# A two-block transformer on one core: gates onto all partitions through DRAM, two norm rows by DMA, four modulation units moved

## The chip, the core and the metric

The kernel runs on one core of one Trainium2 chip. Its engines are TensorE (PE, with its weight loads as PEld), VectorE (DVE), ScalarE (ACT), GpSimd (POOL) and SyncE (SP), beside sixteen DMA engines. The metric is the device time in microseconds, the median of several runs. The profile comes from one profiled execution.

## What is computed

Input x has 256 tokens of width 1024, everything in fp32. Two blocks follow each other.

The first block has two layers. For each layer the conditioning vector c gives six rows of width 1024:

```
mod = silu(c) @ w_ada[layer] + b_ada[layer]
shift_m, scale_m, gate_m, shift_f, scale_f, gate_f = split(mod, 6)
h = rms_norm(x, g_mix) * (1 + scale_m) + shift_m
x = x + gate_m * (concat(conv, sgu, gla, hgrn mixers of h @ w_in) @ w_out)
h = rms_norm(x, g_ffn) * (1 + scale_f) + shift_f
x = x + gate_f * y        # layer 0: swiglu; layer 1: 8 experts, top 2
```

After the second layer comes `rms_norm(x, final_norm_g)`. The second block is a forgetting attention (its norm has the gain `a_norm_2`), a convolutional feed-forward, a sparse attention and a second convolutional feed-forward. The diff touches how the gates `gate_m`, `gate_f` and the two gains `final_norm_g`, `a_norm_2` come onto all 128 partitions, and when the last modulation rows are computed.

## The kernel before, in words

All work is written out in one order, and each engine runs its own instructions in that order. Tokens lie in two tiles of 128 partitions. Every fp32 product is made from a high and a low part of both operands in three matmuls (`mm3`); ScalarE casts the high part of a weight half (L266) and VectorE subtracts it to get the low part (L267). The weights come as units of 1 MB in one stream on SP's queue (`Stream`): six raw buffers, freed in order, and at most four split halves. In the experts four more raw buffers and two row tiles are lent to the stream.

The stages are the first mixers (layer 0), a dense feed-forward, the second mixers (layer 1), the experts, then the second block. `mixers` runs twelve projections of 256 columns (`unit`, `tok_unit`), and between them the chains of the two linear attentions (`linear`), mostly on VectorE and ScalarE. `project` and `close` apply w_out, add the residual and start the next norm; `close` has two gaps in which `fill` is called.

The modulation is computed by `ada(l, g)` for layer l and a third g of the six rows, from eight units of w_ada that are used as they are. One unit is four matmuls with 32 output partitions each (L781). After the eighth unit the group ends: ScalarE copies the PSUM bank into a row (L786), PE transposes it (L789), and VectorE makes shift and scale columns (`modc`, `gs`, L791 and L797). For g > 0 one gate row is left. The tile for it is loaded with the bias on all partitions by a DMA of GpSimd (L370); PE broadcasts the gate from one partition of the row to all 128 by two matmuls with a column of the identity (L806), and VectorE adds each to the bias in place (L809). The gates are read in the residual of `project` and of the feed-forward (L1102), and the last one in the experts' `scatter` (L1419).

Group (0,0) is made at the start. The others, (0,1), (0,2), (1,0), (1,1), (1,2), are 40 units, and `FILL` (L341) says how many are taken at each call of `fill`: the twelve calls of the first mixers, the two gaps after them, the feed-forward, the two gaps after it, the twelve calls of the second mixers. `plan` puts the units' loads into the stream in the same places. A group holds one of the eight PSUM banks from its first unit to its end. Group (1,2) gives the shift and scale that `routing` spreads before the experts, and the gate that the experts use.

Row tiles (tag "row", three of them) hold gates, the decay rows of `linear` (L938, L939), and later the two norm rows. `experts` runs eight experts of seven chunks; at the fifth chunk of the last one it calls `late`, which is `spread` of the two gains: per row eight broadcast matmuls against the identity (L385) and two ScalarE copies (L387). `combined` reads the rows after the last expert (L1620, L1647). GpSimd has little else to do: the routing weights (L1216), four products at the end of the second mixers (L1278) and a few splits (L267).

Of the kernel before, what the change touches and what calls it, by code (L numbers as in the profile page):

```python
# [9 lines left out]
FT = mybir.dt.float32  # L10
# [5 lines left out]
OP = mybir.AluOpType  # L16
AX = mybir.AxisListType
P = 128
T = 256
D = 1024  # L20
# [51 lines left out]
def _vec(v):  # L72
    return np.asarray(v).reshape(-1, P).T
# [44 lines left out]
def vectors(a):  # L118
    c = Cols()
    c.add("c", _vec(a["c"]))  # L120
    for l in range(2):
        c.add(f"mixg{l}", _vec(a["norm_mix_g"][l]))
        c.add(f"bada{l}", _vec(a["b_ada"][l]))
        c.early = c.early or c.n
        c.add(f"ffng{l}", _vec(a["norm_ffn_g"][l]))
        c.add(f"convw{l}", a["conv_w"][l].reshape(3, 2, P).transpose(2, 1, 0))
        c.add(f"glab{l}", _vec(a["gla_b_gate"][l]))
        c.add(f"glag{l}", _twice(a["gla_norm_g"][l]))
        c.add(f"hgg{l}", _twice(a["hgrn_norm_g"][l]))
        c.add(f"lb{l}", _vec(a["hgrn_lower_bounds"][l]))  # L130
        c.add(f"glaw{l}", a["gla_w_gate"][l])
        c.add(f"fb{l}", _vec(a["f_conv_b_2"][l]))
        c.add(f"fw{l}", a["f_conv_w_2"][l].reshape(3, 44, P).transpose(2, 1, 0))
    c.add("fing", _vec(a["final_norm_g"]))
    c.add("ag", _vec(a["a_norm_2"]))
    for n, s in (("aq", "a_q_gain_2"), ("ak", "a_k_gain_2"), ("kc", "kc_gain_2"), ("ks", "ks_gain_2"),
                 ("kw", "kw_gain_2"), ("bq", "b_q_gain_2")):
        c.add(n + "gain", _twice(a[s]))
    f = np.asarray(a["a_b_f_2"]).reshape(16, 1)
    c.add("fbias", np.concatenate([f, np.zeros_like(f), f]))  # L140
    c.add("gbias", np.asarray(a["b_b_gate_2"]).reshape(48, 1))
    for n in ("kc", "vc"):
        c.add(n + "pe", a[n + "_pe_2"].reshape(16, 2, 64).transpose(1, 2, 0).reshape(P, 16))
    return c
# [2 lines left out]
SHAPES = {n: np.zeros(s, np.float32) for n, s in dict(  # L147
    c=(1, D), norm_mix_g=(2, D), norm_ffn_g=(2, D), b_ada=(2, 6 * D), conv_w=(2, 3, 256), gla_b_gate=(2, P),
    gla_norm_g=(2, 64), hgrn_norm_g=(2, 64), hgrn_lower_bounds=(2, 256), gla_w_gate=(2, 16, P), f_conv_b_2=(2, 5632), f_conv_w_2=(2, 3, 5632),
    final_norm_g=(D,), a_norm_2=(1, D), a_q_gain_2=(1, 64), a_k_gain_2=(1, 64), kc_gain_2=(64,), ks_gain_2=(64,), kw_gain_2=(64,), b_q_gain_2=(1, 64),  # L150
    kc_pe_2=(32, 64), vc_pe_2=(32, 64), a_b_f_2=(1, 16), b_b_gate_2=(1, 48)).items()}

EARLY_UP = (0, 11)
# [6 lines left out]
def pack(a):  # L160

    a = {k: np.asarray(v) for k, v in a.items()}
    o = {"x": a["x"].reshape(T, D), "w_ada": a["w_ada"]}
    o["consts"] = constants().array()
    o["vecs"] = vectors(a).array()
    w = a["w_in"]
    o["w_in"] = np.stack([
        np.concatenate([_ws(w[l][:, s + (_PAIRS if s in _FEAT[:2] else np.arange(256))]) for s in _FEAT]
                       + [_ts256(w[l][:, s:s + 256]) for s in _TOK])
        for l in range(2)])  # L170
    o["w_ag"] = np.stack([_kcol(w[l][:, 1792:1808]) for l in range(2)])
    rows = np.concatenate([np.arange(512), 512 + _PAIRS, 768 + _PAIRS])
    o["w_out"] = np.stack([_ts1024(a["w_out"][l][rows]) for l in range(2)])
    o["sgu_w"] = a["sgu_w"].transpose(0, 3, 1, 2)
    o["rows_b"] = a["b_ada"]
    o["sgu_g"] = a["sgu_norm_g"]
    o["sgu_b"] = a["sgu_b"]
    o["bg"], o["fg"] = a["b_norm_2"], a["f_norm_2"]
    o["kvg"] = a["kv_norm_2"].reshape(1, D)
    o["ffn1"], o["ffn3"] = _first256(a["ffn_w1"][0], 0), _first256(a["ffn_w3"][0], 0)  # L180
    o["ffn2"] = _ts1024(a["ffn_w2"][0])
    o["router"] = _kcol(a["moe_router"][0])
    for n in ("1", "3"):
        w = a["moe_w" + n][0].reshape(NE, 2, 4, P, 7, 512).transpose(0, 4, 1, 3, 2, 5)
        o["moe" + n] = w.reshape(NE, 14, P, 2048)
    o["moe2"] = a["moe_w2"][0].reshape(NE, 14, 2, P, D).transpose(0, 1, 3, 2, 4).reshape(NE, 14, P, 2048)
    w = a["a_w_in_2"][0]
    o["a_in"] = np.concatenate([_ws(w[:, :2048]), _ts256(w[:, 2048:3072])])
    o["a_f"] = _kcol(np.concatenate([w[:, 3072:], np.zeros_like(w[:, 3072:]), w[:, 3072:]], 1))
    o["a_out"] = _ts1024(a["a_w_out_2"][0])  # L190
    w = a["kv_w_2"].reshape(D, 6, P)
    o["kv_w"] = np.concatenate([_ts256(w[:, 0:2].reshape(D, 256)), _ws(w[:, [2, 4]].reshape(D, 256)),
                                _ts256(w[:, [3, 5]].reshape(D, 256))])
    for n in ("kc", "vc"):
        o[n + "_w1"] = a[n + "_w1_2"].reshape(16, P, 256).transpose(1, 0, 2)
        o[n + "_w2"] = _kcol(a[n + "_w2_2"])
    w = a["b_w_in_2"][0]
    o["b_in"] = _ws(w[:, :D].reshape(D, 2, 8, 64).transpose(0, 2, 1, 3).reshape(D, D))
    o["b_g"] = _kcol(w[:, D:])
    o["b_out"] = _ts1024(a["b_w_out_2"][0].reshape(2, 8, 64, D).transpose(1, 0, 2, 3).reshape(D, D))  # L200
    w = a["f_w_up_2"]
    o["f_up"] = np.stack([_first256(w[l], *EARLY_UP) for l in range(2)])
    o["f_dn"] = np.stack([_ts1024(a["f_w_down_2"][l]) for l in range(2)])
    o["pos"] = a["positions_2"].reshape(1, T)
    return {k: np.ascontiguousarray(v) for k, v in o.items()}
# [132 lines left out]
class Core:  # L338
    TAIL = 4

    FILL = [1, 1, 1, 1, 1, 1, 1, 2, 2, 2, 2, 1], [2, 2], [0] * 2 + [1] * 16 + [0] * 4, [2, 2], [0] * 12  # L341

    def __init__(self, ctx, tc, a, out, stop=None):
        self.ctx, self.tc, self.nc, self.a, self.out, self.stop = ctx, tc, tc.nc, a, out, stop
        pool = lambda name, **k: ctx.enter_context(tc.tile_pool(name=name, **k))
        self.raw = pool("raw", bufs=Stream.RAW)
        self.split = pool("split", bufs=Stream.SPLIT)
        self.keep = pool("keep", bufs=1)
        self.nrm = pool("nrm", bufs=1)
        self.part = ExitStack()  # L350
        self.mine = self.part.enter_context(tc.tile_pool(name="first", bufs=1, side="right"))
        self.psum = pool("psum", bufs=8, space=bass.MemoryType.PSUM)
        self.s = Stream(self.nc, self.raw, self.split)
        self.names = 0
        self.open = self.between = None
        self.own = None
# [8 lines left out]
    def row(self, ap):  # L365

        self.names += 1
        t = self.mine.tile([P, D], FT, name=f"row{self.names}", tag="row", bufs=3)
        if ap is not None:
            self.nc.gpsimd.dma_start(t, ap.partition_broadcast(P).rearrange("p a d -> p (a d)"))  # L370
        return t

    def warm(self, n):

# [395 lines left out]
    def ada(self, l, g):  # L770

        nc = self.nc
        ps = self.ps("ada")
        for k in range(8):
            if k < 7:
                t, = self.s.whole()
            else:
                with self.s.quiet():
                    t, = self.s.whole()
            for j in range(4):  # L780
                nc.tensor.matmul(ps[32 * j:32 * j + 32, :], self.cT[:, k:k + 1].to_broadcast([P, 32]), t[:, j * 512:(j + 1) * 512],  # L781
                                 start=k == 0, stop=k == 7)
            if k < 7:
                yield
        row = self.rows()[1][:, :512]
        nc.scalar.copy(row, ps)  # L786
        tr = self.ps("adt")
        for b in range(4):
# [1 line left out]
        o = 16 * g  # L790
# [3 lines left out]
        if g == 0 or g == 2:  # L794
            n = g // 2
# [2 lines left out]
                                           self.vv(("mixg", "ffng")[n] + str(l)), op0=OP.add, op1=OP.mult)  # L798
        if g > 0:

            v = 2 if g == 1 else 5
            j0 = 0 if g == 1 else 2
            gate = self.row(self.a["rows_b"][l:l + 1, v * D:(v + 1) * D])
            for h in range(2):
                gp = self.ps("gate")
                nc.tensor.matmul(gp, self.cc("ident")[:, 32 * (j0 + h):32 * (j0 + h) + 1].to_broadcast([P, P]), row,  # L806
                                 start=True, stop=True)
                c = slice(h * 512, (h + 1) * 512)
                nc.vector.tensor_tensor(gate[:, c], gp, gate[:, c], op=OP.add)  # L809
            self.gate[l, g] = gate  # L810
        yield

# [1456 lines left out]
    def run(self):  # L2269
        nc, tc, a, s = self.nc, self.tc, self.a, self.s  # L2270
# [7 lines left out]
        first = self.normed(self.feats(self.gs[:, 0, 0], self.modc[:, 0, 0:8], 1))  # L2278
# [21 lines left out]
        for l in range(2):  # L2300
# [7 lines left out]
            rows = self.project(y, self.gate[l, 1], then, (2, 3, 0, 1, 6, 7, 4, 5), between, gap=fill, close=self.close_routed if l else None)  # L2308
# [15 lines left out]
                nc.scalar.dma_start(self.router, a["router"])  # L2324
        first = self.late
        done, last = self.combined(*first)
        self.experts(*rows, lambda: [self.spread(r, self.vv(n)) for r, n in zip(first, ("fing", "ag"))], done)
        if self.stopped("ffn1"):
            return
        self.phase("fox", c64=8, c1024=4, c1536=8, c2048=12, c8192=3, spare=((8192, 1), (2048, 3)))  # L2330
# [11 lines left out]
        rows = self.conv_ffn(0, self.feats(self.row(a["kvg"]), early=2), kT)  # L2342
# [33 lines left out]
```

## Time and profile before

| | |
|---|---|
| median of 3 runs | 2280.06 us (2277.39 to 2282.93) |
| profiled execution, its own time | 2279.25 us |
| its span, first to last instruction | 2277.5 us |
| instructions | 34045 |
| PE busy | 2206.2 us (97%) |
| DVE busy | 1749.1 us (77%) |
| ACT busy | 1409.4 us (62%) |
| POOL busy | 66.8 us (3%) |
| HBM read | 580.76 MB, 255 GB/s over the span |

Times in the views count from the start of the span. Busy is the time in which an engine executes; idle before an instruction is put down to what released it last. A matmul's record is longer than the time for which it keeps the next one waiting, since matmuls are pipelined: the spacing of starts tells what one costs. An fp32 matmul shows as two records.

### The profile page before, as it was taken

How to read it: one execution, taken by the hardware profiler on the slowest of the kernel's cores; microseconds unless marked ns; L12 is line 12 of the kernel's file. 1: busy time of each engine (PE TensorE's matmuls, PEld its weight loads, DVE VectorE, ACT ScalarE, POOL GpSimd, SP SyncE). 2: the span in 40 equal slices, each digit the busy share in tenths (PEclk: the TensorE clock that was granted, in tenths of full speed). 3: DMA queues.
4: the chain of work that ended last, by engine and by line, in shares of the span. 5: the costliest groups of instructions: out<-in, count | busy, mean ns of one | idle time of the engine just before them, and what ended most of it. 6: DMA issues, size and time to landing. Idle time of an engine off the chain costs nothing. (4 is left out here: it accounts for less than half of the span.)

```text
span 2277.5 us, 34045 instructions
## 1 busy us (share of the span) xinstructions
PE 2206.2 (97%) x13348; PEld 1841.1 (81%) x13348; DVE 1749.1 (77%) x2284; ACT 1409.4 (62%) x1956; POOL 66.8 (3%) x104
## 2 busy tenths in 40 slices
PE   6999999999999999999999999998999999999999
PEld 4777888887887878787887878786888998779998
DVE  3675445586989899989999899887677777676776
ACT  3544334545877777777777777676665556555554
POOL 1000000001000000000000000001004000100000
PEclk9999999999999999999999999999999999999999
DMA  9767766535999999999999999686334555313451
GB/s 394 274 243 288 271 246 219 196 105 209 359 369 348 347 339 365 348 354 347 350 367 352 337 350 362 231 342 242 130 112 160 204 185 193 132 38 130 167 191 68
DMA packets 87560, 584.35 MB, mean 257 GB/s; under 512 B 9984, under 2 KB 11648, under 8 KB 20960
## 3 DMA queue, kind: packets, MB, share of 16 engines
q1 hardware_dynamic: 84096, 575.22, 68.2%
q0 software_dynamic: 1296, 4.59, 0.6%
q8 instruction: 106, 1.74, 0.3%
q10 hardware_dynamic: 2000, 2.29, 0.3%
q14 instruction: 62, 0.51, 0.1%
HBM read 580.76 MB, written 1.05 MB: 255 GB/s over the span
## 5 line engine op out<-in xcount | busy, mean ns | idle before, releaser
L267 DVE TENSOR_TENSOR lo<-raw,hi 128x1024 fp32r<-128x1024 f32 x695 | 834.5, 1225 | 292.5 <-ACT hi L266 282.6
L266 ACT CAST hi<-raw 128x1024 fp32r<-128x1024 f32 x698 | 719.7, 1050 | 328.2 <-PE fu L441 152.2
L440 PE MATMUL fu<-hTh,hi 128*128 128x256 f32 x1440 | 413.1, 287 | 2.0 <-DVE lst L933 1.2
L442 PE MATMUL fu<-hTh,lo 128*128 128x256 f32 x1440 | 408.0, 283 | 0.8 <-DVE lo L267 0.8
L441 PE MATMUL fu<-hTl,hi 128*128 128x256 f32 x1440 | 407.8, 283 | 0.0
L440 PE MATMUL h<-hi,xh 128*128 128x512 f32 x896 | 361.1, 403 | 4.3 <-PEq L1521 4.2
L441 PE MATMUL h<-lo,xh 128*128 128x512 f32 x896 | 354.4, 396 | 4.5 <-DVE lo L267 4.5
L442 PE MATMUL h<-hi,xl 128*128 128x512 f32 x896 | 354.8, 396 | 0.0
L440 PEld LDWEIGHTS fu<-hTh,hi 128*128 128x128 f32 x1440 | 274.1, 190 | 17.3 <-issue 12.2
L441 PEld LDWEIGHTS fu<-hTl,hi 128*128 128x128 f32 x1440 | 272.5, 189 | 3.2 <-issue 2.2
L267 DVE TENSOR_TENSOR lo<-more,hi 128x1024 fp32r<-128x1024 f32 x216 | 258.1, 1222 | 21.3 <-ACT hi L266 18.3
L442 PEld LDWEIGHTS fu<-hTh,lo 128*128 128x128 f32 x1440 | 272.0, 189 | 1.0 <-DVE lo L267 1.0
L266 ACT CAST hi<-more 128x1024 fp32r<-128x1024 f32 x216 | 224.1, 1052 | 44.3 <-PE h L442 22.4
L441 PEld LDWEIGHTS h<-lo,xh 128*128 128x128 f32 x896 | 168.9, 189 | 45.2 <-DVE lo L267 7.9
L440 PEld LDWEIGHTS h<-hi,xh 128*128 128x128 f32 x896 | 168.8, 188 | 41.9 <-ACT yh L1421 4.7
L442 PEld LDWEIGHTS h<-hi,xl 128*128 128x128 f32 x896 | 168.6, 188 | 41.3
L440 PE MATMUL y<-hi,egh 128*128 128x512 f32 x448 | 177.4, 396 | 0.7 <-ACT egh L454 0.7
L442 PE MATMUL y<-hi,egl 128*128 128x512 f32 x448 | 177.4, 396 | 0.0
L441 PE MATMUL y<-lo,egh 128*128 128x512 f32 x448 | 176.4, 394 | 0.8 <-DVE lo L267 0.8
L441 PE MATMUL acc<-lo,gh 128*128 128x512 f32 x264 | 104.6, 396 | 1.7 <-DVE lo L267 1.7
L440 PE MATMUL acc<-hi,gh 128*128 128x512 f32 x264 | 106.1, 402 | 0.0
L442 PE MATMUL acc<-hi,gl 128*128 128x512 f32 x264 | 104.4, 396 | 0.0
(502 smaller groups left out, 3057.1 us busy)
## 6 DMA issues: line engine op xcount, KB each, us to landing
raw<-in_moe_dram SPq DMA_DIRECT2D x201, 1024.0 KB, 6.9
more<-in_moe_dram SPq DMA_DIRECT2D x108, 1024.0 KB, 7.0
raw<-in_w_ada_dram SPq DMA_DIRECT2D x48, 1024.0 KB, 6.7
raw<-in_f_up_dram SPq DMA_DIRECT2D x44, 1024.0 KB, 4.9
raw<-in_ffn_dram SPq DMA_DIRECT2D x33, 1024.0 KB, 5.6
row<-in_moe_dram SPq DMA_DIRECT2D x54, 512.0 KB, 7.1
raw<-in_w_in_dram SPq DMA_DIRECT2D x24, 1024.0 KB, 6.9
raw<-in_f_dn_dram SPq DMA_DIRECT2D x22, 1024.0 KB, 5.5
```

The source lines that it names most:

```text
L266: self.nc.scalar.copy(hi, src)
L267: (self.nc.gpsimd if pool else self.nc.vector).tensor_tensor(lo, src, hi.bitcast(FT), op=OP.subtract)
L440: t.matmul(out, a[0], b[0], start=start, stop=False)
L441: t.matmul(out, a[0], b[1], start=False, stop=False)
L442: t.matmul(out, a[1], b[0], start=False, stop=stop)
```

## The change

Three things change.

Each gate's two broadcast matmuls and two VectorE adds go. The row tile of `ada` has a second half of 512 columns; two DMAs on GpSimd's queue load the gate's bias into it, each onto 32 partitions. GpSimd adds the row (64 partitions by 512). Two more DMAs of GpSimd store one partition of each half into a line of 1024 in DRAM, and a last one loads that line onto all 128 partitions of the gate's tile (`row`).

The two norm gains leave the table of vectors and become two rows of an input of their own. At the fifth chunk of the last expert `late` issues one broadcast load for each, on GpSimd's queue, where `spread` had its matmuls and copies.

In `FILL` four units leave the feed-forward (sixteen single units become twelve) and go to the second mixers: one at the eighth call of `fill`, two at the ninth, one at the eleventh. So the two gaps after the feed-forward hold the first four units of group (1,2), not the last four, and the group ends in the second mixers.

```
--- before.py
+++ after.py
@@ -131,8 +131,6 @@
         c.add(f"glaw{l}", a["gla_w_gate"][l])
         c.add(f"fb{l}", _vec(a["f_conv_b_2"][l]))
         c.add(f"fw{l}", a["f_conv_w_2"][l].reshape(3, 44, P).transpose(2, 1, 0))
-    c.add("fing", _vec(a["final_norm_g"]))
-    c.add("ag", _vec(a["a_norm_2"]))
     for n, s in (("aq", "a_q_gain_2"), ("ak", "a_k_gain_2"), ("kc", "kc_gain_2"), ("ks", "ks_gain_2"),
                  ("kw", "kw_gain_2"), ("bq", "b_q_gain_2")):
         c.add(n + "gain", _twice(a[s]))
@@ -147,7 +145,7 @@
 SHAPES = {n: np.zeros(s, np.float32) for n, s in dict(
     c=(1, D), norm_mix_g=(2, D), norm_ffn_g=(2, D), b_ada=(2, 6 * D), conv_w=(2, 3, 256), gla_b_gate=(2, P),
     gla_norm_g=(2, 64), hgrn_norm_g=(2, 64), hgrn_lower_bounds=(2, 256), gla_w_gate=(2, 16, P), f_conv_b_2=(2, 5632), f_conv_w_2=(2, 3, 5632),
-    final_norm_g=(D,), a_norm_2=(1, D), a_q_gain_2=(1, 64), a_k_gain_2=(1, 64), kc_gain_2=(64,), ks_gain_2=(64,), kw_gain_2=(64,), b_q_gain_2=(1, 64),
+    a_q_gain_2=(1, 64), a_k_gain_2=(1, 64), kc_gain_2=(64,), ks_gain_2=(64,), kw_gain_2=(64,), b_q_gain_2=(1, 64),
     kc_pe_2=(32, 64), vc_pe_2=(32, 64), a_b_f_2=(1, 16), b_b_gate_2=(1, 48)).items()}
 
 EARLY_UP = (0, 11)
@@ -173,6 +171,7 @@
     o["w_out"] = np.stack([_ts1024(a["w_out"][l][rows]) for l in range(2)])
     o["sgu_w"] = a["sgu_w"].transpose(0, 3, 1, 2)
     o["rows_b"] = a["b_ada"]
+    o["rows_late"] = np.concatenate([a["final_norm_g"].reshape(1, D), a["a_norm_2"].reshape(1, D)])
     o["sgu_g"] = a["sgu_norm_g"]
     o["sgu_b"] = a["sgu_b"]
     o["bg"], o["fg"] = a["b_norm_2"], a["f_norm_2"]
@@ -338,7 +337,7 @@
 class Core:
     TAIL = 4
 
-    FILL = [1, 1, 1, 1, 1, 1, 1, 2, 2, 2, 2, 1], [2, 2], [0] * 2 + [1] * 16 + [0] * 4, [2, 2], [0] * 12
+    FILL = [1, 1, 1, 1, 1, 1, 1, 2, 2, 2, 2, 1], [2, 2], [0] * 2 + [1] * 12 + [0] * 8, [2, 2], [0] * 7 + [1, 2, 0, 1, 0]
 
     def __init__(self, ctx, tc, a, out, stop=None):
         self.ctx, self.tc, self.nc, self.a, self.out, self.stop = ctx, tc, tc.nc, a, out, stop
@@ -350,6 +349,7 @@
         self.part = ExitStack()
         self.mine = self.part.enter_context(tc.tile_pool(name="first", bufs=1, side="right"))
         self.psum = pool("psum", bufs=8, space=bass.MemoryType.PSUM)
+        self.dram = pool("dram", bufs=1, space=bass.MemoryType.DRAM)
         self.s = Stream(self.nc, self.raw, self.split)
         self.names = 0
         self.open = self.between = None
@@ -367,8 +367,11 @@
         self.names += 1
         t = self.mine.tile([P, D], FT, name=f"row{self.names}", tag="row", bufs=3)
         if ap is not None:
-            self.nc.gpsimd.dma_start(t, ap.partition_broadcast(P).rearrange("p a d -> p (a d)"))
+            self.row_into(t, ap)
         return t
+
+    def row_into(self, t, ap):
+        self.nc.gpsimd.dma_start(t, ap.partition_broadcast(P).rearrange("p a d -> p (a d)"))
 
     def warm(self, n):
 
@@ -782,7 +785,8 @@
                                  start=k == 0, stop=k == 7)
             if k < 7:
                 yield
-        row = self.rows()[1][:, :512]
+        t = self.rows()[1]
+        row, bias = t[:, :512], t[:, 512:]
         nc.scalar.copy(row, ps)
         tr = self.ps("adt")
         for b in range(4):
@@ -798,15 +802,18 @@
                                            self.vv(("mixg", "ffng")[n] + str(l)), op0=OP.add, op1=OP.mult)
         if g > 0:
 
-            v = 2 if g == 1 else 5
-            j0 = 0 if g == 1 else 2
-            gate = self.row(self.a["rows_b"][l:l + 1, v * D:(v + 1) * D])
+            v, j0 = (2, 0) if g == 1 else (5, 2)
+            b = slice(32 * j0, 32 * j0 + 64)
             for h in range(2):
-                gp = self.ps("gate")
-                nc.tensor.matmul(gp, self.cc("ident")[:, 32 * (j0 + h):32 * (j0 + h) + 1].to_broadcast([P, P]), row,
-                                 start=True, stop=True)
-                c = slice(h * 512, (h + 1) * 512)
-                nc.vector.tensor_tensor(gate[:, c], gp, gate[:, c], op=OP.add)
+                c = v * D + h * 512
+                nc.gpsimd.dma_start(bias[32 * (j0 + h):32 * (j0 + h) + 32],
+                                    self.a["rows_b"][l:l + 1, c:c + 512].partition_broadcast(32).rearrange("p a d -> p (a d)"))
+            nc.gpsimd.tensor_tensor(bias[b], bias[b], row[b], op=OP.add)
+            self.names += 1
+            line = self.dram.tile([1, D], FT, name=f"line{self.names}")
+            for h in range(2):
+                nc.gpsimd.dma_start(line[:, h * 512:(h + 1) * 512], bias[32 * (j0 + h):32 * (j0 + h) + 1])
+            gate = self.row(line)
             self.gate[l, g] = gate
         yield
 
@@ -2324,7 +2331,7 @@
                 nc.scalar.dma_start(self.router, a["router"])
         first = self.late
         done, last = self.combined(*first)
-        self.experts(*rows, lambda: [self.spread(r, self.vv(n)) for r, n in zip(first, ("fing", "ag"))], done)
+        self.experts(*rows, lambda: [self.row_into(r, a["rows_late"][i:i + 1]) for i, r in enumerate(first)], done)
         if self.stopped("ffn1"):
             return
         self.phase("fox", c64=8, c1024=4, c1536=8, c2048=12, c8192=3, spare=((8192, 1), (2048, 3)))
```

## Rows read from the trace of the kernel before

**Rows 1.** The page: busy time, share of the span, instructions, by engine.

```profile
PE 2206.2 (97%) x13348; PEld 1841.1 (81%) x13348; DVE 1749.1 (77%) x2284; ACT 1409.4 (62%) x1956; POOL 66.8 (3%) x104
```

**Rows 2.** Stretches: busy us of PE, PEld, DVE, ACT, POOL; clock; DMA share; GB/s.

```profile
270.00:300.00 30.00, 30.00 (x217) 25.66 (x217) 15.45 (x16) 10.33 (x11) 0.00 (x0) 1.00 0.70 254
450.00:480.00 30.00, 25.22 (x255) 23.51 (x255) 26.29 (x47) 16.99 (x30) 0.74 (x1) 0.94 0.31 106
1520.00:1540.00 20.00, 20.00 (x106) 16.85 (x105) 14.77 (x14) 14.69 (x19) 0.00 (x0) 1.00 0.79 300
```

**Rows 3.** Timeline of PE, end of group (1,1): start, duration (us), instruction.

```profile
303.72 1.07 PE L781 MATMUL ada<-raw,cT 128*32 128x512 f32 x8
...
305.98 1.88 PE L806 MATMUL gate<-xn,consts 128*128 128x512 f32 x4
...
307.30 0.80 PE L440 MATMUL acc<-hi,gh 128*128 128x512 f32 x1
```

**Rows 4.** Timeline of PE, end of group (0,2).

```profile
147.46 1.88 PE L806 MATMUL gate<-xn,consts 128*128 128x512 f32 x4
```

**Rows 5.** Timeline of PE, end of group (0,1).

```profile
100.41 3.14 PE L806 MATMUL gate<-xn,consts 128*128 128x512 f32 x4
...
103.48 1.45 PE L781 MATMUL ada<-raw,cT 128*32 128x512 f32 x8
```

**Rows 6.** DMA issues of the whole run: count, KB each, median us to landing.

```profile
raw<-in_w_ada_dram SPq DMA_DIRECT2D x48, 1024.0 KB, 6.7
...
row<-in_rows_b_dram POOLq DMA_DIRECT2D x4, 512.0 KB, 7.6
```

**Rows 7.** Row tiles: count, duration ns min/median/max, first and last start (us).

```profile
L1102 DVE TENSOR_TENSOR xn<-acc,row x12: 672/684/692, 170.8 to 542.7; 128x512 f32<-128x512 f32 x12
...
L1620 DVE TENSOR_TENSOR xn<-x,row x2: 681/1229/1777, 1570.6 to 1573.4; 128x512 f32<-128x512 f32 x2
```

**Rows 8.** Timeline of POOL, end of the second mixers.

```profile
531.81 1.28 POOL L1278 TENSOR_TENSOR xn<-x,gr 128x512 f32<-128x512 f32 x1 [58.71 <-issue]
...
546.88 2.50 POOL L267 TENSOR_TENSOR lo<-raw,hi 128x1024 fp32r<-128x1024 f32 x1 [1.42 <-ACT hi L266]
```

**Rows 9.** Timeline of DVE, the same stretch.

```profile
536.84 1.42 DVE L1258 SCALAR_TENSOR_TENSOR xn<-xn,st,sr 128x512 f32<-128x512 f32 x2
...
546.41 3.50 DVE L1258 SCALAR_TENSOR_TENSOR xn<-xn,st,sr 128x512 f32<-128x512 f32 x2
```

**Rows 10.** Timeline of PE, the two norm rows.

```profile
1521.59 3.73 PE L385 MATMUL row<-consts,vecs 128*128 128x128 f32 x32
```

**Rows 11.** Timeline of PE, a lone unit in the feed-forward.

```profile
345.57 1.06 PE L781 MATMUL ada<-raw,cT 128*32 128x512 f32 x8
...
346.57 0.50 PE L440 MATMUL acc<-hi,gh 128*128 128x512 f32 x1
```

**Rows 12.** Timeline, PE and DVE, gap before the second mixers.

```profile
410.57 1.92 PE L781 MATMUL ada<-raw,cT 128*32 128x512 f32 x16
...
416.22 0.42 DVE L508 CAST hTh<-tf 128x512 fp32r<-128x512 f32 x1
...
416.69 0.39 PE L440 MATMUL tu<-sp,hTh 128*128 128x256 f32 x1 [1.12 <-DVE hTh L508]
```

**Rows 13.** Timeline of PE, the same gap before the feed-forward.

```profile
189.74 1.92 PE L781 MATMUL ada<-raw,cT 128*32 128x512 f32 x16
...
191.59 0.38 PE L440 MATMUL tu<-sp,hTh 128*128 128x256 f32 x1
```

**Rows 14.** Waits of PE, 425 to 545: us in total, times, longest.

```profile
PE lsc L897 <- ACT lst L935: 2.0, 1, 2.0
...
PE fu L440 <- DVE lst L933: 1.2, 1, 1.2
...
PE lsc L897 <- DVE vn L1043: 0.8, 1, 0.8
```

**Rows 15.** Stretch 477 to 483, columns as in Rows 2.

```profile
477.00:483.00 6.00, 5.92 (x27) 5.92 (x28) 5.81 (x8) 4.83 (x7) 0.00 (x0) 0.50 0.16 26
```

More of the change, by code (lines that the diff above doesn't have):

```diff
@@ L133, in vectors @@
         c.add(f"fw{l}", a["f_conv_w_2"][l].reshape(3, 44, P).transpose(2, 1, 0))
-    c.add("fing", _vec(a["final_norm_g"]))
-    c.add("ag", _vec(a["a_norm_2"]))
     for n, s in (("aq", "a_q_gain_2"), ("ak", "a_k_gain_2"), ("kc", "kc_gain_2"), ("ks", "ks_gain_2"),
@@ L149 @@
     gla_norm_g=(2, 64), hgrn_norm_g=(2, 64), hgrn_lower_bounds=(2, 256), gla_w_gate=(2, 16, P), f_conv_b_2=(2, 5632), f_conv_w_2=(2, 3, 5632),
-    final_norm_g=(D,), a_norm_2=(1, D), a_q_gain_2=(1, 64), a_k_gain_2=(1, 64), kc_gain_2=(64,), ks_gain_2=(64,), kw_gain_2=(64,), b_q_gain_2=(1, 64),
+    a_q_gain_2=(1, 64), a_k_gain_2=(1, 64), kc_gain_2=(64,), ks_gain_2=(64,), kw_gain_2=(64,), b_q_gain_2=(1, 64),
     kc_pe_2=(32, 64), vc_pe_2=(32, 64), a_b_f_2=(1, 16), b_b_gate_2=(1, 48)).items()}
@@ L175, in pack @@
     o["rows_b"] = a["b_ada"]
+    o["rows_late"] = np.concatenate([a["final_norm_g"].reshape(1, D), a["a_norm_2"].reshape(1, D)])
     o["sgu_g"] = a["sgu_norm_g"]
@@ L339 @@
     TAIL = 4
-    FILL = [1, 1, 1, 1, 1, 1, 1, 2, 2, 2, 2, 1], [2, 2], [0] * 2 + [1] * 16 + [0] * 4, [2, 2], [0] * 12
+    FILL = [1, 1, 1, 1, 1, 1, 1, 2, 2, 2, 2, 1], [2, 2], [0] * 2 + [1] * 12 + [0] * 8, [2, 2], [0] * 7 + [1, 2, 0, 1, 0]
     def __init__(self, ctx, tc, a, out, stop=None):
@@ L352, in __init__ @@
         self.psum = pool("psum", bufs=8, space=bass.MemoryType.PSUM)
+        self.dram = pool("dram", bufs=1, space=bass.MemoryType.DRAM)
         self.s = Stream(self.nc, self.raw, self.split)
@@ L369, in row, with row_into @@
         if ap is not None:
-            self.nc.gpsimd.dma_start(t, ap.partition_broadcast(P).rearrange("p a d -> p (a d)"))
+            self.row_into(t, ap)
         return t
+    def row_into(self, t, ap):
+        self.nc.gpsimd.dma_start(t, ap.partition_broadcast(P).rearrange("p a d -> p (a d)"))
     def warm(self, n):
@@ L784, in ada @@
                 yield
-        row = self.rows()[1][:, :512]
+        t = self.rows()[1]
+        row, bias = t[:, :512], t[:, 512:]
         nc.scalar.copy(row, ps)
@@ L799, in ada @@
         if g > 0:
-            v = 2 if g == 1 else 5
-            j0 = 0 if g == 1 else 2
-            gate = self.row(self.a["rows_b"][l:l + 1, v * D:(v + 1) * D])
+            v, j0 = (2, 0) if g == 1 else (5, 2)
+            b = slice(32 * j0, 32 * j0 + 64)
             for h in range(2):
[L805 to L809, printed above, removed]
+                c = v * D + h * 512
+                nc.gpsimd.dma_start(bias[32 * (j0 + h):32 * (j0 + h) + 32],
+                                    self.a["rows_b"][l:l + 1, c:c + 512].partition_broadcast(32).rearrange("p a d -> p (a d)"))
+            nc.gpsimd.tensor_tensor(bias[b], bias[b], row[b], op=OP.add)
+            self.names += 1
+            line = self.dram.tile([1, D], FT, name=f"line{self.names}")
+            for h in range(2):
+                nc.gpsimd.dma_start(line[:, h * 512:(h + 1) * 512], bias[32 * (j0 + h):32 * (j0 + h) + 1])
+            gate = self.row(line)
             self.gate[l, g] = gate
@@ L2326, in run @@
         done, last = self.combined(*first)
-        self.experts(*rows, lambda: [self.spread(r, self.vv(n)) for r, n in zip(first, ("fing", "ag"))], done)
+        self.experts(*rows, lambda: [self.row_into(r, a["rows_late"][i:i + 1]) for i, r in enumerate(first)], done)
         if self.stopped("ffn1"):
```

## The prediction

> **What bounds the kernel now.** I read the page's busy times first. TensorE (PE) is busy for 97% of the 2277.5 us span [rows 1]. So a microsecond of PE work that goes is worth up to a microsecond, but only where PE and nothing else sets the pace. The view by stretches settles where [rows 2]. In the dense feed-forward of layer 0 (270 to 300) PE is busy for 30.00 of 30 us with DMA at 0.70. In the last expert (1520 to 1540) it is busy for 20.00 of 20. In the middle of the second mixers (450 to 480) it is busy for 25.22 of 30, while VectorE (DVE) has 26.29 and DMA 0.31: there DVE's long chain leads, and PE has holes. The timelines of PE, DVE and GpSimd (POOL) then priced the edited places. All sums are made against the profiled execution, 2279.25 us with a span of 2277.5; the median of the three runs shown is 0.81 us above it.
>
> **Gates, on PE.** Each of four gate blocks loses its two broadcast matmuls (four records). In the feed-forward, for unit group (1,1), they start at 305.98; the next matmul starts at 307.30 but lasts 0.80 where the neighbours of its kind last 0.40, so they hold PE for 1.32 + 0.40 = 1.72 us [rows 3]. The block of group (0,2) has the same four records in the same 1.88 us [rows 4]. The block of (0,1) takes 100.41 to 103.48, 3.07 us [rows 5], since it falls in slow clock and the next unit then waits; slow-clock work removed need not give back its full time, because what follows moves into the same slow stretch, so I take 1.72 there too. Three blocks: 5.16 us. Ends: 1.72, if in the first mixers DVE leads as it does in the second, and 6.5, with 3.07 for (0,1). The fourth block is counted below, in its gap.
>
> **Gates, on the new path.** One gate now needs two small bias loads, one POOL add (64x512), two row stores to DRAM and one 512 KB broadcast load, all on POOL's queue. The nearest POOL row is a 128x512 tensor_tensor, 1.28 us [rows 8]. No row shows a POOL store to DRAM: I bound its landing by 0 and by the broadcast load's 7.6 us [rows 6]. From the copy of the row to a ready gate that is 1.28 + 0 to 7.6 + 7.6 = 9 to 17 us. The first gate, begun near 100, would be there by 117 and is first read at 170.8 [rows 7], so over 50 us cover it. The gate of (1,2) is begun near 500, after the eleventh projection of the second mixers, and is read only in the experts. Behind its waits on POOL stand the routing weights and the product that started at 531.81 [rows 8]; POOL issues the last load by about 500 + 1.28 + 7.6 = 509, some 20 us earlier. So I cost the path at nothing. Without that cover each late gate would cost its lateness whole.
>
> The DVE side loses eight adds that read PSUM and gains contention. While POOL ran a 128x1024 subtraction for 2.50 us [rows 8], two DVE operations took 3.50 us that took 1.42 ten microseconds earlier [rows 9], 2.08 more. A POOL add can so push DVE by up to about its own 1.28 us, and that is a loss only where DVE leads: once, in the second mixers. I take 0 and keep 1.3 for the range; all four adds on the path are a rival below.
>
> **The two norm rows.** At the fifth chunk of the last expert 32 matmul records go, 3.73 us in one block with nothing idle before them [rows 10]. PE is full there [rows 2], so I take 3.5 (0.23 of the record is the usual overlap with the next matmul); ScalarE also loses four copies. Two 512 KB loads replace them; POOL has nothing else to do there and each lands in about 7.6 us [rows 6], while the rows are first read at 1570.6 [rows 7]. If the loads were in the way of the weights, the price would be 1 MB at 300 GB/s [rows 2], 3.5 us, and the term would be 0.
>
> **Four units out of the feed-forward.** A lone unit holds PE from 345.57 to 346.57 [rows 11], 1.00 us. Four: 4.0 us, in a stage where PE is full. The 1 MB load of each moves on SP's queue from among the feed-forward's weights to among the mixers' input weights, where DMA has more room [rows 2].
>
> **The gap before the second mixers.** Two units stay in it, but group (1,2) no longer ends there. Now the units start at 410.57 and PE resumes at 416.69, because DVE's cast of the normed tile, at 416.22, stands behind the group's own DVE work, which waits for its transposes and gate matmuls [rows 12]. The same gap before the feed-forward has two units and no end of a group: 189.74 to 191.59, 1.85 us, no wait after it [rows 13]. So 6.12 - 1.85 = 4.27 us go, the fourth gate block among them.
>
> **The second mixers.** The last unit now ends its group there: from its start to where the gate matmuls began was 305.98 - 303.72 = 2.26 us [rows 3], in a part where PE is full. The other three fall just before and after the gated unit's second projection, where PE waited 2.0, 1.2 and 0.8 us for PSUM banks that DVE and ScalarE release [rows 14]. That is 4.0 us of holes for 3.0 of work. But the group holds one of the eight banks meanwhile, and the units call for splits earlier in DVE's queue. I charge 1.0 us in all. Ends: nothing, and 3.0 + 2.0 (nothing hidden and the longest bank wait a second time).
>
> **Sum.** 5.16 + 3.5 + 4.0 + 4.27 = 16.9 gained, 2.26 + 1.0 = 3.3 given back: 13.7 us. From the profiled time that is 2265.6, from the median 2266.4; I forecast 2266 us. Low end of the gain: 1.72 + 0 + 4.0 + 4.27 - 2.26 - 5.0 - 1.3 = 1.4 us. High end: 6.5 + 3.5 + 4.0 + 4.27 - 2.26 = 16.0, and 19.0 with the clock below.
>
> **Rivals.**
> - *The second mixers take the units at full price.* DVE leads, a bank is gone, one more wait of 2.0 appears and the POOL add holds DVE for 1.3: given back 2.26 + 5.0 + 1.3 = 8.6, net gain 8.3, 2271 us. For it: DVE at 26.29 of 30 [rows 2]. Against: the holes are larger than the work [rows 14].
> [...]
> - *POOL's adds on the path.* Each of the four holds DVE, and PE behind it, for its 1.28 us [rows 8, 9]: 5.1 us back, 2271 us. For it: the stretched pair. Against: at three of the four places PE, not DVE, is the one waited for. [...]
> - *Slower: loads exposed in the second mixers.* Raw buffers are freed in order, so an unused unit holds back all loads behind it. A unit's load takes 6.7 us to land [rows 6]; if PE waits a whole landing at each of the four, that is 26.8 us, net 13.1 slower, 2293 us. It decides from 13.7 / 4 = 3.4 us of wait per unit. Against: pairs of units run without such a wait in both gaps [rows 12, 13], and DMA is at 0.31.
> - *The PE time is not the pace.* The first mixers give 0, the norm rows are hidden anyway, and the second mixers take all: gain 1.4, 2278 us, no change that counts. For it: only the stretch by DVE in the second mixers.
>
> **How the numbers follow.** Forecast 0.57 (its own range 2262 to 2269), full price 0.15, clock 0.11, POOL's adds 0.04, no pace 0.08, exposed loads 0.05. The range 2258 to 2274 holds the first four: the high end of the gain from the median is 2261, less the 3 us by which the runs shown scatter; at the other end 2271 with the same 3. It leaves out the last two, 0.13. A change under 0.2% (4.6 us) cannot be told from none. Faster than that: the first four cases, 0.87. Within: no pace, 0.07 of its 0.08. Slower: the exposed loads and the rest, 0.06.
>
> **What would show it.** In the profile after: no gate matmuls, so lo, acc and unit records follow the transposes directly at all places; the gap before the second mixers at about 1.9 us from its units to the next projection; the MoE's last chunks without a break at the fifth; modulation matmuls in the second mixers, the last followed by one short wait for ScalarE. The waits of PE there should stay near 4 us in sum. Wrong would be: a DMA wait of PE at a w_ada or w_in load in the second mixers; any wait of a residual product for the gate's load; DVE operations stretched to twice their time beside POOL's adds with PE idle behind them; a longer stretch at clock 0.50.

## The result, and the profile after

The changed kernel takes 2256.17 us (median of six runs, 2255.23 to 2257.96); the kernel before takes 2277.9 in the runs beside it. The ratio is 0.9898, 95% interval 0.9888 to 0.9908: faster by 21 to 26 us by the interval. The forecast was 2266 with a range of 2258 to 2274: the direction was right, but the gain was some 9 us larger than the sum allowed for. The profiled executions say the same: 2279.25 us before, 2256.06 after, spans 2277.5 and 2254.3, so 23.2 us.

First the page's row of busy times, which answers to [rows 1].

```profile
PE 2182.4 (97%) x13300; PEld 1824.5 (81%) x13300; DVE 1746.2 (77%) x2276; ACT 1406.9 (62%) x1952; POOL 82.8 (4%) x126
```

PE lost 48 records (16 of gates, 32 of norm rows) and 23.8 us of busy time. The two norm rows were one block of 3.73 us [rows 10]; the gates' records were four blocks, three of 1.88 and one of 3.14 [rows 3 to 5], 8.8 us. That leaves 11 us by which the records that stayed keep PE busy for less time. At the edited places the trace looks as the prediction said. PE's timeline at the end of group (1,1) and in the gap before the second mixers (start, duration in us, instruction):

```profile
295.15 1.06 PE L784 MATMUL ada<-raw,cT 128*32 128x512 f32 x8
296.93 0.66 PE L793 MATMUL adt<-consts,xn 128*128 128x128 f32 x4 [0.71 <-ACT xn L790]
297.33 0.48 PE L443 MATMUL acc<-hi,gh 128*128 128x512 f32 x1
...
394.30 1.92 PE L784 MATMUL ada<-raw,cT 128*32 128x512 f32 x16
396.15 0.38 PE L443 MATMUL tu<-sp,hTh 128*128 128x256 f32 x1
```

No gate block stands between the transposes and the next acc matmul, which lasts 0.48 us and not 0.80 [rows 3]. The gap is 396.15 - 394.30 = 1.85 us, where it was 6.12 [rows 12]. Next, the longest waits of PE in the second mixers, 404 to 528 (us in total, times, longest):

```profile
PE lsc L904 <- ACT lst L942: 1.9, 1, 1.9
PE lsc L904 <- DVE lst L940: 1.1, 1, 1.1
PE lg L1248 <- DVE logit L1252: 0.9, 1, 0.9
PE adt L793 <- ACT xn L790: 0.7, 1, 0.7
PE lt L895 <- DVE vn L1050: 0.4, 1, 0.4
```

The three waits of [rows 14] are 1.9, 1.1 and 0.4 now, and the one new wait is the group's end, 0.7. No load of w_ada or w_in is among them. On POOL the first gate goes like this, and the add of the third lasts 1.27 us:

```profile
98.35 1.81 POOL L811 TENSOR_TENSOR xn<-xn 64x512 f32<-64x512 f32 x1 [59.38 <-ACT xn L790]
100.45 1.01 POOL L815 DMA_DIRECT2D line<-xn  x2 [0.29 <-POOL xn L811]
103.09 0.56 POOL L374 DMA_DIRECT2D row<-line  x1 [1.62 <-DMA line<-xn]
...
296.95 1.27 POOL L811 TENSOR_TENSOR xn<-xn 64x512 f32<-64x512 f32 x1 [113.53 <-ACT xn L790]
```

Of the DMA issues (count, KB each, median us to landing) two rows belong to it:

```profile
row<-line POOLq DMA_DIRECT2D x4, 512.0 KB, 4.0
...
line<-xn POOLq DMA_DIRECT2D x8, 2.0 KB, 3.2
```

The broadcast goes out 4.7 us after the add began and takes about 4.0 to land, so the gate is there near 107, some 57 us before its first use at 163.8.

So where did the rest come from? Aligning PE's matmuls of the two traces by order shows the lead growing at the edits, but also steadily, by about 0.026 of the time, wherever the feature projections run (fu: weights against the normed, transposed tokens hTh and hTl). From 1577 to 1891 of the trace before, where no edit lies, it grows from 20.3 to 24.8 us. The timeline of PE in one such unit, the 4th and the 94th of its 96 matmuls, of the kernel before and then of the one after:

```profile
2157.52 0.28 PE L440 MATMUL fu<-hTh,hi 128*128 128x256 f32 x1
...
2168.32 0.28 PE L440 MATMUL fu<-hTh,hi 128*128 128x256 f32 x1
```

```profile
2136.18 0.28 PE L443 MATMUL fu<-hTh,hi 128*128 128x256 f32 x1
...
2146.68 0.28 PE L443 MATMUL fu<-hTh,hi 128*128 128x256 f32 x1
```

Ninety matmuls take 10.80 us before and 10.50 after: 120.0 and 116.7 ns each. The durations of single records (0.28) hide this; the starts show it. Over the whole run I took every distance below 160 ns between the starts of two consecutive matmuls into fu, called feature matmuls from here on, some 4220 in each trace: the mean is 119.9 ns before and 116.8 after. That is 3.1 ns on each of 4220 matmuls, 13 us of PE time in code that no line of the diff touches.

What the diff does touch is an address. The table vecs loses 16 columns (the two norm rows), 64 bytes in every partition, and hTh, hTl and all tiles allocated behind it lie 64 bytes lower. In the compiled programs hTh starts at byte 115424 of each partition before and at 115360 after; hi and lo, the split weights, keep their places (all at 128 within 256 bytes). These absolute addresses are read from the compiled programs and stand in no view of the profile; what follows needs only by how much each run moves a tile.

### The profile page after: what moved, and what is told of

The parts are those of the page before. It is cut to its first block, busy times and chain, and to the rows that moved or that the text cites. A ratio compares the mean times of both kernels' runs of the same rounds, so it can differ in the third digit from the quotient of the medians.

```text
span 2254.3 us, 33997 instructions
## 1 busy us (share of the span) xinstructions
PE 2182.4 (97%) x13300; PEld 1824.5 (81%) x13300; DVE 1746.2 (77%) x2276; ACT 1406.9 (62%) x1952; POOL 82.8 (4%) x126
## 5 line engine op out<-in xcount | busy, mean ns | idle before, releaser
L265 ACT CAST hi<-raw 128x1024 fp32r<-128x1024 f32 x698 | 719.7, 1050 | 316.3 <-PE fu L444 140.3
L444 PE MATMUL fu<-hTl,hi 128*128 128x256 f32 x1440 | 402.8, 280 | 0.0
L445 PE MATMUL fu<-hTh,lo 128*128 128x256 f32 x1440 | 402.7, 280 | 0.1
L265 ACT CAST hi<-more 128x1024 fp32r<-128x1024 f32 x216 | 223.7, 1050 | 44.6 <-PE h L445 22.6
```

The source lines that it names most:

```text
L265: self.nc.scalar.copy(hi, src)
L444: t.matmul(out, a[0], b[1], start=False, stop=False)
L445: t.matmul(out, a[1], b[0], start=False, stop=stop)
```

## Experiments

Theory P (place): the pace of the feature matmuls goes by the address of hTh and hTl. Rival E (edits): fewer transposes, gates or loads beside them let them run faster. An idle tile, which is never read or written, moves what is allocated behind it and nothing else. Each run stands beside runs of the kernel before on the same chip, which took 2277.3 to 2280.1 us (medians). "Spacing" is the mean described above.

**b_shift64 and a_shift64.** The same edit, on the kernel before and on the one after:

```diff
+        keep.tile([P, 16], FT, name="pad")
         self.hT = (keep.tile([P, 8, T], FR, name="hTh"), keep.tile([P, 8, T], FR, name="hTl"))
```

> The kernel before, with one idle tile of 16 columns (64 bytes per partition) between the table vecs and the tile hTh. Nothing else changes; the address of hTh and hTl within 128 bytes becomes that of the kernel after (32 instead of 96). Place theory: the 4320 feature matmuls that move hTh and hTl as 128x256 follow each other every 116.8 ns instead of 119.9, 3.1 x 4290 = up to 13 us, so 2265 to 2268 us against 2278. Rival (the edits themselves free the feature matmuls, by fewer transposes, gates or loads beside them): spacing 119.9 and 2278 us.

> The kernel after, with the same idle tile of 16 columns between vecs and hTh, so that every address behind it is that of the kernel before. Place theory: spacing 119.9 ns again, 10 to 13 us slower than after, 2266 to 2269 us, which is what the prediction's own terms gave (2266). Rival (the edits): spacing stays 116.8 and the time 2256 us.

a_shift64: 2265.47 us, ratio 0.9939 (0.9925 to 0.9953), spacing 119.9. With the old addresses back, the changed kernel takes what was forecast, and the feature matmuls have the pace of before to a tenth of a ns. So the edits and the addresses are two separate gains: 13.9 us by the ratio (10.7 to 17.1), and 2265.5 - 2256.2 = 9.3 us. E falls. b_shift64: 2275.52 us, 0.9992 (0.9983 to 1.0001), spacing 118.4: here P's forecast (2265 to 2268) missed. The place within 128 bytes is the same as after (32), the pace is not. So P held, but not with a period of 128.

**a_shift32 and a_shift96.** As a_shift64, with 8 and 24 columns.

> The kernel after with an idle tile of 8 columns (32 bytes) there: hTh at 64 within 128 bytes. Place theory: the spacing is one of its own, since it depends on the address; 117 to 120 ns and 2256 to 2269 us, faster than 2256 if 64 is a better place than 32. Rival: 2256 us.

> The kernel after with an idle tile of 24 columns (96 bytes) there: hTh at 0 within 128 bytes. Place theory: aligned should be the best or equal to the best place: 2250 to 2256 us, spacing at most 116.8 ns; rival: 2256 us as after.

2255.55 us (0.9899, 0.9883 to 0.9914) with 117.4 ns, and 2263.77 (0.9940, 0.9926 to 0.9953) with 119.0. The second was a miss of mine: hTh at a multiple of 256 is not the best place but one of the worse.

**The parts alone**, addresses as before: only_gates has the diff's gate lines without the rest; only_units its line of `FILL`; only_rows the two DMAs, with the 16 columns left unread in vecs.

```diff
-        self.experts(*rows, lambda: [self.spread(r, self.vv(n)) for r, n in zip(first, ("fing", "ag"))], done)
+        self.experts(*rows, lambda: [self.row_into(r, a["rows_late"][i:i + 1]) for i, r in enumerate(first)], done)
```

> The kernel before with the gates alone changed (bias on GpSimd, through DRAM); the table vecs, the norm rows and the order of the units stay, so no address behind vecs moves. The prediction's terms: three blocks of 1.72 us in full PE time, 5.2 us, ends 1.7 and 6.5, and the fourth, in the gap before the second mixers, only as far as DVE's queue ends earlier (0 to 1.7). So 2271 to 2276 us against 2277.5, feature spacing 119.9. Rival (GpSimd's adds hold DVE on the path, 4 x 1.28): 2277 us.

> The kernel before with the order of the units alone changed (four of them out of the feed-forward into the second mixers); gates on PE, vecs and norm rows stay, so no address behind vecs moves. The prediction's terms: 4.0 out of the feed-forward, 4.27 out of the gap, given back 2.26 + 1.0 and the gate block that now stands in the mixers, 1.7: net 3.3 us, 2274 us. Rival of units at full price: net -2 us, 2279 us. Feature spacing 119.9.

> The kernel before with the two norm rows alone fetched by DMA instead of spread by matmuls; the 16 columns stay in vecs, unread, so no address behind vecs moves. The prediction's term: 3.5 us, 2274 us, feature spacing 119.9; if the loads stand in the way of weights: 2277.5 us.

only_gates: 2272.57 us, 0.9971 (0.9959 to 0.9982), 6.6 us. only_units: 2275.82, 0.9987 (0.9978 to 0.9996), 3.0 us. only_rows: 2276.21, 0.9987 (0.9978 to 0.9996), 3.0 us. Spacing 119.9 in all three. Each of these gains is known to 2 or 3 us only. They add up to 12.6, and the three edits together gave 13.9 (a_shift64): within that, the edits don't depend on each other, and none of them is the missing gain.

**a_back64.** The idle tile behind hTl, so that only hTh and hTl are at the addresses of after.

```diff
         self.hT = (keep.tile([P, 8, T], FR, name="hTh"), keep.tile([P, 8, T], FR, name="hTl"))
+        keep.tile([P, 16], FT, name="padb")
```

> The kernel after with the idle tile of 16 columns behind hTl instead of in front of hTh: hTh and hTl stay at the addresses of the kernel after, every tile behind them has the address of the kernel before. Place theory with hT as the cause: spacing 116.8 and 2256 us. Rival (another tile behind them is the cause): 119.9 and 2265 us as with the idle tile in front.

2257.04 us (0.9900, 0.9884 to 0.9916), spacing 116.8. For the mean spacing of the feature matmuls it is hTh and hTl, and no tile behind them.

**a_shift160, a_shift192, a_shift256, a_place128.** 40 and 48 columns in front of hTh; identb (256 bytes) moved in front of it; and hTh and hTl in front of vecs behind 32 idle columns.

```diff
+        self.identb = keep.tile([P, P], BF, name="identb")
         self.hT = (keep.tile([P, 8, T], FR, name="hTh"), keep.tile([P, 8, T], FR, name="hTl"))
-        self.identb = keep.tile([P, P], BF, name="identb")
```

> The kernel after with an idle tile of 40 columns (160 bytes) between vecs and hTh: hTh at 64 within 256 bytes. The shifts so far gave, by place within 256: 160: 116.8, 192: 117.3, 224: 119.9, 0: 119.1, 32: 118.4 ns between feature matmuls. If the pace goes by the place within 256 bytes and changes smoothly, 64 is near 118 ns, 2260 us; if it goes by 128 bytes it is 117.3 as at 192, 2256 us.

> The kernel after with an idle tile of 48 columns (192 bytes): hTh at 96 within 256 bytes. By a smooth course within 256 bytes between 32 (118.4) and 160 (116.8): about 117.5 ns and 2258 us; by the place within 128 bytes it would be as at 224: 119.9 ns and 2266 us.

> The kernel after with the tile identb moved from behind hTl to in front of hTh: hTh and hTl 256 bytes further, nothing else moved. If the pace goes by the place within 256 bytes: 116.8 ns and 2256 us as after. If it goes by the distance to some other tile or a longer period: another spacing, up to 119.9 ns and 2266 us.

> The kernel after with hTh and hTl in front of vecs instead of behind it and an idle tile of 32 columns ahead of them: hTh at 128 within 256 bytes. By the place within 256 bytes it lies between 96 and 160 and should be near 116.8 ns, 2256 us, or better; by a longer period anything from 116 to 120 ns, 2253 to 2266 us.

a_shift256 repeats after: 116.85 ns, 2256.54 us (0.9905, 0.9888 to 0.9921), which speaks for a period of 256 bytes (or a divisor of it that the other places then rule out). The smooth course fell, and with it two of my forecasts: a_shift192 has 118.3 ns and 2261.47 us (0.9930, 0.9913 to 0.9946), a_place128 119.9 and 2265.14 (0.9951, 0.9933 to 0.9968), but a_shift160 114.5 and **2246.45 us (0.9857, 0.9841 to 0.9874)**, faster than both kernels.

**a_far64, a_split64, a_split128, b_shift96.** Is it hT's own place that counts, or its place against the weight tiles that the same matmuls use? a_far64 brings hTh to place 64 at a distant address; a_split64 keeps that very address and moves hi and lo by 64 bytes; a_split128 moves them by 128, with hTh again at 64. b_shift96 is the kernel before with 24 idle columns.

```diff
         self.split = pool("split", bufs=Stream.SPLIT)
+        self.split.tile([P, 16], FT, name="pads", tag="pads", bufs=1)
```

> The kernel after with hTh and hTl in front of vecs and an idle tile of 16 columns ahead of them: place 64 within 256 bytes as in a_shift160 (2246.5 us, about 114.5 ns), but 3328 bytes lower. If the place within 256 bytes sets the pace: about 114.5 ns and 2246 us. If a longer period or the distance to a tile other than hi and lo sets it: another value, 117 to 120 ns and 2256 to 2266 us.

> As a_far64, hTh and hTl at the very same address, but with the idle tile of 16 columns in the pool of hi and lo, so that all weight tiles (hi, lo) lie 64 bytes further (192 within 256 instead of 128). If hT's own place sets the pace: as a_far64, about 114.5 ns. If the place of hT against hi and lo sets it: the difference is now that of a_shift96 (hT at 0, hi at 128), so about 119 ns and 8 us or more slower than a_far64. The matmuls of the experts (h and y, 232 to 235 ns), which read hi and lo, may change as well, by up to some ns on 4000 of them.

> The kernel before with an idle tile of 24 columns (96 bytes) between vecs and hTh: place 64 within 256 bytes, the very address of a_shift160, and none of the edits. Place theory: the edits were worth 11.8 us (a_shift64) and the place 19.0 (a_shift160 against a_shift64), so 2278 - 19 = 2259 us, as much as the whole change gained. If place and edits hang together: anywhere between 2259 and 2278.

> The kernel after with hi and lo 128 bytes further (0 within 256) and hTh and hTl at 64 within 256, ahead of consts. If hT's own place sets the pace: about 114.5 ns, 2246 us. If its place against hi and lo does: the difference is 64, that of a_shift192 less 32 and of a_shift64 more 32 (224 - 128 = 96 gave 119.9, 192 - 128 = 64 gave 117.3): 117.3 ns, 2256 us. The matmuls of the experts may change with hi and lo too.

a_far64: 2247.16 us (0.9856, 0.9841 to 0.9871); a_split64: 2270.87 (0.9963, 0.9949 to 0.9977); a_split128: 2257.72 (0.9905, 0.9890 to 0.9921). a_far64 fits both readings; a_split64 and a_split128 came out as the second says. With "difference" for the place of hTh less that of hi and lo, within 256 bytes:

| difference | kernels: spacing in ns (median us) |
|---|---|
| 0 | a_place128 119.9 (2265.1) |
| 32 | after 116.8 (2256.2), a_back64 116.8 (2257.0), a_shift256 116.9 (2256.5) |
| 64 | a_shift32 117.4 (2255.6), **a_split128 117.3 (2257.7)** |
| 96 | before 119.9 (2277.9), a_shift64 119.9 (2265.5), the parts 119.9 |
| 128 | a_shift96 119.0 (2263.8), **a_split64 119.3 (2270.9)** |
| 160 | b_shift64 118.4 (2275.5) |
| 192 | a_shift160 114.5 (2246.5), a_far64 114.3 (2247.2), b_shift96 114.4 (2259.9) |
| 224 | a_shift192 118.3 (2261.5) |

a_far64 and a_split64 have hTh at one and the same address and differ by 5.0 ns and 23.7 us; what moved is hi and lo, and x and consts behind them, which the feature matmuls don't read. Equal differences give equal mean spacings, to 0.3 ns, at places that have nothing else in common; differences 0, 160 and 224 rest on one kernel each. The unit shown above reads, in a_shift160, a_split64 and a_split128:

```profile
2131.10 0.28 PE L443 MATMUL fu<-hTh,hi 128*128 128x256 f32 x1
...
2141.30 0.28 PE L443 MATMUL fu<-hTh,hi 128*128 128x256 f32 x1
```

```profile
2149.00 0.28 PE L444 MATMUL fu<-hTh,hi 128*128 128x256 f32 x1
...
2159.80 0.28 PE L444 MATMUL fu<-hTh,hi 128*128 128x256 f32 x1
```

```profile
2135.33 0.28 PE L444 MATMUL fu<-hTh,hi 128*128 128x256 f32 x1
...
2145.93 0.28 PE L444 MATMUL fu<-hTh,hi 128*128 128x256 f32 x1
```

Ninety matmuls in 10.20, 10.80 and 10.60 us: 113.3, 120.0 and 117.8 ns. b_shift96 is the plainest proof: one idle tile, no edit, 2259.93 us, ratio 0.9909 (0.9895 to 0.9922), nearly as much as the whole change. a_split64 is some 5 us slower than a_shift96 at the same difference, by their ratios (0.9963 and 0.9940; the two ran beside different runs of before). The h and y matmuls of the experts are slower in it by 0.8 ns (their operands' places against hi moved too), which over 3860 of them is 3.1 us, and its feature matmuls by 0.3 ns, 1.3 us; the rest is within the intervals.

The feature matmuls are not the only ones that move. The token projections (tu<-sp,hT) stream the tile sp, which lies behind hTl, against hTh and hTl as loaded weights: their mean spacing is 114.3 to 115.4 ns in before, after and a_shift64, and 119.7 in a_back64, where sp moved and hTh and hTl did not. In a_shift32 the matmuls into acc (512 columns, some 1050 distances) start every 228.4 ns, in all other kernels every 232.4 to 234.0. That is about 5 us, more than the 2.5 us by which its feature matmuls are slower than those of after, so it can account for a_shift32 being as fast; which tile's place does it was not tried.

## Why the prediction was wrong, step by step

**The step that failed is the norm rows' price.** "The two norm rows" counted 32 matmul records and two loads, and counted what the diff takes out of vecs as nothing. Those 16 columns are the 64 bytes that move hTh and hTl. So the same edit is worth 3.5 us by its matmuls, as priced (3.0 by the median of only_rows), and 9.3 us more by the address (after against a_shift64). More generally, the sum held every matmul that isn't edited to its pace of before; at 97% PE [rows 1], 3.1 ns on each of 4220 matmuls are 13 us, and 9.3 of them reached the time. No rival had it, and so the range ended at 2258.

**The other steps hold**, best seen in a_shift64, which has the addresses of before. The lead of its PE over that of the kernel before, at the same matmul in both traces:

| up to (time before, us) | lead, us | step: gained | forecast |
|---|---|---|---|
| 90.11 | 0.35 | no edit: 0.4 | 0 |
| 105.58 | 2.23 | gate (0,1): 1.9 | 1.72 |
| 131.60 | 3.49 | no edit: 1.3 | 0 |
| 149.18 | 5.19 | gate (0,2): 1.7 | 1.72 |
| 307.94 | 6.86 | gate (1,1): 1.7 | 1.72 |
| 346.90 | 11.61 | four units: 4.8 | 4.0 |
| 416.69 | 15.83 | gap: 4.2 | 4.27 |
| 498.25 | 12.15 | second mixers: -3.7 | -3.26 |
| 1499.92 | 11.88 | experts: -0.3 | 0 |
| 1525.08 | 15.38 | norm rows: 3.5 | 3.5 |
| 1577.35 | 15.47 | end of the experts: 0.1 | 0 |

Without the 1.6 us that stand at no edit, this is 13.9 us; the forecast was 13.7.

- *Gates:* as priced. The lead is read behind the long acc matmul (0.80 us in [rows 3]), which belongs to the block. At (0,1) PE first gains 2.5 us; then the 64 lkv matmuls, which took 1.21 us before, take 1.83 at the lower clock (1.67 in after, where the granted clock is 0.50 from 99 to 102) and give 0.6 back. This is why the prediction held the 3.07 of [rows 5], where the clock of before is 0.50 from 101 to 104, to 1.72. The 1.3 us between the first two blocks is not the gates': from 128 to 132 the kernel before is at granted clock 0.57, where the same work of a_shift64 is at 1.00, and only_rows, which has no edit up to there, is at 1.00 too and gains 1.0 us.
- *Units:* 1.2 each against 1.00 [rows 11]; the hand-over on both sides of a unit goes with it. In before the unit's first matmul starts 0.21 us after the last one into fu, where those follow each other by 0.12, and the acc matmul behind it holds PE for 0.33 us, the next ones for 0.23.
- *Gap and norm rows:* as priced. In the last expert of after PE has no break at the fifth chunk. The two loads were not issued there: they stand at the fifth chunk in program order, but GpSimd issued them as soon as a VectorE split had freed their tiles, at 1420.8 and 1422.0, some 80 us earlier. DMA moves 368 GB/s in this stretch (it was at 300 [rows 2]):

```profile
1503.00:1523.00 20.00, 20.00 (x90) 16.13 (x88) 18.18 (x17) 15.48 (x17) 0.00 (x0) 1.00 0.97 368
```

- *Given back in the second mixers:* 3.7, in after 20.54 - 17.39 = 3.15. The rival of full price (8.6) falls, and so does that of exposed loads.
- *The clock:* the 3.0 us between 16.0 and 19.0 at the high end, and with them the chance of 0.11, were an estimate of mine; no run shows that term. In before, feature matmuls start every 0.213 us at granted clock 0.50 (477.5 to 482.8) and every 0.120 at 1.00, by which the 6 us of [rows 15] would give some 2.6. Nor did the stretch at the slower level go: it comes earlier, in the waits of 1.9 and 1.1 us, but it is there, at 0.54 from 453 to 460 of after beside 0.50 in [rows 15], and a second one follows (0.58 from 470 to 474). So one sign of being wrong, a longer stretch at clock 0.50, did show. Its cost is small, a mean clock of 0.96 over the second mixers (404 to 528) against 0.97 before (425 to 545), and it isn't the edits': b_shift96, which has none, is at 0.95 there.

```profile
453.00:460.00 7.00, 4.62 (x24) 4.11 (x25) 6.71 (x7) 5.15 (x8) 0.00 (x0) 0.54 0.78 310
```

- *POOL's adds on the path:* the first add, in the lines of POOL above, lasts 1.81 us where the one of (1,1) lasts 1.27, and beside it runs a DVE subtraction of 1.91 that took 1.22 just before:

```profile
97.81 1.22 DVE L266 TENSOR_TENSOR lo<-raw,hi 128x1024 fp32r<-128x1024 f32 x1 [0.81 <-ACT hi L265]
99.24 0.17 DVE L795 TENSOR_TENSOR modc<-adt,vecs 128x16 f32<-128x16 f32 x1 [0.20 <-PE adt L793]
99.34 1.91 DVE L266 TENSOR_TENSOR lo<-raw,hi 128x1024 fp32r<-128x1024 f32 x1
```

The stretch was foreseen, and no loss of PE shows at it: the step gained what was priced. What makes the subtraction longer beside the add (1.91 for 1.22 us) was not tried. TensorE's own pace changes too, by up to 5.6 ns in 120 (114.3 to 119.9), with how its two operands lie to each other, in kernels whose other engines do the same work.

**A loss that no step had.** In the part from 1940 to 2060, where no edit lies, the profiled executions of after and of a_shift64 lose 4 to 6 us of their lead again. Two stretches of after show why:

```profile
1952.00:1956.00 4.00, 4.00 (x20) 3.75 (x20) 2.88 (x11) 3.25 (x15) 0.00 (x0) 0.57 0.00 0
2010.00:2017.00 7.00, 7.00 (x28) 6.25 (x27) 2.15 (x6) 3.35 (x10) 1.62 (x2) 0.51 0.14 25
```

PE is busy throughout, at the lower clock level for most of the time (a mean of 0.57 and 0.51; [rows 15] has 0.50); before the first PE was busy for 4.74 of 6 us, before the second for 5.23 of 7. In the trace of before the mean clock over these 120 us is 1.00; it is 0.96 in after, 1.00 in only_units, 0.99 in a_back64, 0.97 in only_gates and only_rows, 0.96 in a_shift160 and 0.94 in a_shift64, so it varies without order. The edits are neither needed for it nor enough: b_shift96, without any, has 0.96, and a_shift192 and a_place128, with all of them, have 1.00. What brings it on stays open. The balance of the profiled executions is then: 15.4 by the steps, some 12 by the feature matmuls' pace, less 4 here, 23.

## What to carry to other kernels

A line that only shortens a table can move the operands of the busiest matmuls, so list which tiles lie behind a resized one, and compare the starts of consecutive matmuls, not their durations, before crediting a gain to an edit. An idle tile in front of an operand is a cheap experiment: it tells the place from the edit, and here one tile (b_shift96, 20.7 us by the ratio) was worth more than the three edits (13.9). Keep the good place in the version that stays: with 160 idle bytes the changed kernel takes 2246.45 us instead of 2256.17.

## What the runs showed of the hardware

- TensorE's pace at full clock (granted 1.00) depends on where the streamed and the loaded operand of the fp32r feature matmuls lie to each other, with a period of 256 bytes as far as tried (116.85 ns in a_shift256, 116.8 in after): 114.3 to 119.9 ns for 256 columns. The means of the ten placements of the changed kernel with hi and lo unmoved run from 114.3 ns and 2247.2 us to 119.9 and 2265.5, about 3.4 us for each ns.
- Within a unit the mean spacing takes few values, to a few tenths of a ns: 113.3, 116.7, 117.3, 117.8, 118.3, 118.7 and 120.0 ns. At difference 192 most units run at 113.3 and some at 117.8 in the same run; what decides between the two was not tried. In after 4 of 53 units run at 117.8, in a_back64 8 of 53, so tiles behind hTl can have a part in it. Nor was it shown what makes the difference: the two reads of TensorE, or the writing of hi and lo, whose places move with them.
- Each feature matmul has a weight load of its own (4320 of both in after). For 256 columns 113.3 ns is the least that any unit shows, and the address decides how much more it is, up to 120.0.
- The experts' matmuls did not change with the edits or the idle tiles: 233.2 to 233.4 ns for h and y in all kernels in which hi and lo stay.
